# Stores on POOL's queue, gate weights a chunk ahead, four gate buffers in the merge: a one-core transformer block

## The chip, the core and the metric

The kernel runs on one core of one Trainium2 chip. A core has a matrix engine (TensorE, here PE, with its weight loads shown as PEld), three elementwise engines (VectorE = DVE, ScalarE = ACT, GpSimd = POOL) and a fifth that issues transfers only (SyncE = SP). Each engine takes its own instructions strictly in order; engines wait for each other on semaphores. Transfers (DMAs) are issued by an engine, in its order, and then run beside it. The metric is device time in microseconds for one execution, lower is better.

## The reference, cut to what matters

One block on x of 512 positions by 1024 channels, all in float32:

```python
h = rmsnorm(x, norm_mix_g)
z = h @ w_in                                   # 1024 x 7184
uv = gelu(z[:, :2048]); z_u, z_v = uv[:, :1024], uv[:, 1024:]
q, k, v, f_logit = ...                         # 3 x 1024 columns, then 16
gates = sigmoid(z[:, 5136:])                   # gate_a, gate_b: 1024 columns each
a = z_u * (W_s @ layernorm(z_v) + b_s)         # W_s: 8 groups, 128 x 128, inside blocks of 128 positions
b = forgetting_attention(q, k, v, f_logit)     # 16 heads; cum = cumsum(log_sigmoid(f_logit + b_f))
x = x + (gate_a * (a @ w_branch_a) + gate_b * (b @ w_branch_b)) @ w_out
x = x + (gelu(conv(h2 @ w_up)[:, :2816]) * conv(h2 @ w_up)[:, 2816:]) @ w_down   # h2 = rmsnorm(x)
x = x + (p @ w_ple) * sigmoid(rmsnorm(x) @ w_ple_gate)
return rmsnorm(x)
```

## The kernel before, in words

**Products.** Every float32 product is made of three products of rounded parts. `load_w` loads a weight tile of 128 x 1024 floats into a raw buffer (L141, a DMA issued by SP), ACT casts it to its high part `whi` (L144), and DVE, or POOL where `sub=G`, subtracts that to get the low part `wlo` (L145). `split_out` does the same to a result (L366 on ACT, L367 on DVE). A product then runs three matmuls per 128 rows: `wlo` with the high part of the activation (L167, L153, L227, L299 are the first of three in their product functions), and two more.

**Buffers.** Raw weights go in turn through a ring of three buffers `raw` and, until the attention, five more called `more`. The high and low parts have rings of their own. A load is issued when its buffer is free.

**Stages.** (1) Norm of x; V, first half; the forget gate's logits (L568, 16 matmuls) from a weight that is cast by DVE (L561) and whose low part DVE makes (L562); V, second half. The cumulated log of the forget gate goes to DRAM (`cum_d`, L591), and comes back in the attention, spread over partitions. DVE and ACT also form four sums of quarters of h (L607 and splits into S1 to S4), for the next stage. (2) A chunk of gates (`gate_steps(0)`: 24 matmuls, then ACT copies the result and a store puts it into `gate_d`, L642), then z_v and z_u by two Winograd-Strassen products of seven quarter products each (P1, P7, P6, P2, P5, P4, P3; L299 to L306), whose weight quarters are loaded by L267 and combined on DVE (L272). (3) The mix: one gate chunk as cover, and then eight groups `mix(g)`: split of the normalised z_v, three matmuls, product with z_u (L724), four transposes (L729), split into the halves of S4h or S4l in turn, and two stores to `aT_d` (L733); between them, as fill, the matmuls of three more gate chunks. (4) The attention over eight pairs of heads, with the q and k of later pairs and nine more gate chunks as fill. POOL clears two K tiles (kz, L772 and L773) and adds the mask to `cum` (md, L804). (5) The merge: for each chunk of the b branch, load gate (L967), sigmoid (L968), product, multiply (L980), store to `gyb_d` (L981); then the a branch likewise (multiply L991), with the stored b part loaded (L993), added on POOL (L994) and split into mT. Gate tiles have two buffers `sg`. (6) w_out, the feed-forward part, the end.

**What sets the order.** On PE it is the order of the code in these stages (`manual_schedule`), with `weave` putting fill between items. On the other engines a list scheduler with its own estimate of times orders the instructions, so that a change in one place may move instructions elsewhere.

Of the kernel before, what the change touches and what calls it, by code (L numbers as in the profile page):

```python
# [9 lines left out]
F32 = mybir.dt.float32  # L10
F32R = mybir.dt.float32r
AF = mybir.ActivationFunctionType
# [3 lines left out]
P = 128  # L16
S = 512
# [26 lines left out]
def hybrid_block(  # L44
# [27 lines left out]
    def uid(s):  # L72
        state["n"] += 1
        return f"{s}_{state['n']}"
# [55 lines left out]
    def more_tile():  # L130
        return state["more"].tile([P, D], F32, tag="more", name=uid("more"), bufs=X_BUFS)
# [104 lines left out]
    def steps(g, n):  # L236
        for _ in range(n):
            next(g)
# [349 lines left out]
    V.tensor_tensor(fbb[:, 1:, :], fbb[:, 1:, :], tot[0:16, 0:15, None].broadcast_to([16, 15, 32]),  # L588
                    ALU.add)
    cum_d = tc.dram_tile([16, S], F32, name="cum_d")  # L590
    nc.sync.dma_start(cum_d, fb)  # L591


    maskb = consts.tile([P, P], F32, tag="maskb", name="maskb")
# [37 lines left out]
    def gate_weights(n):  # L632
        return load_w(w_in_v[:, :, gate_col(n):gate_col(n) + P], 8, P)

    def gate_steps(n, tag, place, w=None):

        w = w or gate_weights(n)
        bk = bank(tag)
        yield from proj_T_steps([(*w, 0, 8, 0)], hT, bk)
        t = place()  # L640
        A.copy(t, bk)
        nc.sync.dma_start(gate_d[n * P:n * P + P, :], t)  # L642
# [19 lines left out]
    def chain(*gs):  # L662
        for g in gs:
            yield from g
# [1 line left out]
    bsT = ph.tile([P, NK], F32, tag="bsT", name="bsT")  # L666
    aT_d = [tc.dram_tile([D, S], F32, name=f"aT_d{t}") for t in range(2)]
    with tc.manual_schedule(engines={ET.PE}):
        run(gate_steps(0, "mm", lambda: more_tile()[:, 0:512]))
        units = wino_steps(wino_jobs(w_in_v, 1024, hT, sums, wino_rows(zv, gelu_zv))  # L670
                           + wino_jobs(w_in_v, 0, hT, sums, wino_rows(zu, gelu_zu)))
        steps(units, 168)
        gb = [more_tile(), more_tile()]
        nc.sync.dma_start(gb[0], rows_bc(ln_g[0], D))
        nc.sync.dma_start(gb[1], rows_bc(ln_b[0], D))

        wst = more_tile().rearrange("p (g s) -> p g s", g=8)
        nc.sync.dma_start(wst, w_s[0].rearrange("g t s -> t g s"))
        G.memset(wst[0:64, :, 64:128], 0.0)
        bsr = ph.tile([P, P], F32, tag="bsr", name="bsr")  # L680
        G.memset(bsr, 0.0)
        nc.sync.dma_start(bsr[0:8, :], b_s[0])
        steps(units, 24)

        nm, va = tiny("nm", NB), tiny("va", NB)
        V.tensor_tensor(nm, zs[:, 0:NB], zs[:, NB:], ALU.add)
        V.tensor_scalar(nm, nm, -1.0 / D, None, ALU.mult)
        sq = tiny("sq", 2 * NB, 1)
        for rb in range(NB):
            A.activation(zv[:, rb, :], zv[:, rb, :], AF.Identity, bias=nm[:, rb:rb + 1])  # L690
            for h in range(2):
                A.activation(bank("mm"), zv[:, rb, 512 * h:512 * h + 512], AF.Square,
                             accum_out=sq[:, NB * h + rb:NB * h + rb + 1])
        V.tensor_tensor(va, sq[:, 0:NB], sq[:, NB:], ALU.add)
        V.tensor_scalar(va, va, 1.0 / D, EPS, ALU.mult, ALU.add)
        y = rsqrt_of(va, NB)
        for rb in range(NB):
            V.scalar_tensor_tensor(zv[:, rb, :], zv[:, rb, :], y[:, rb:rb + 1], gb[0],
                                   ALU.mult, ALU.mult)
            V.tensor_tensor(zv[:, rb, :], zv[:, rb, :], gb[1], ALU.add)  # L700
        steps(units, 120)

        wsT = [quarter(f"S1{t}").rearrange("p (g t) -> p g t", g=8) for t in "hl"]
        bk = bank("mm")
        T.transpose(bk[:, 0:P], bsr, ident)
        V.tensor_copy(bsT, bk[:, 0:NK])
        steps(units, 12)
        for g0 in (0, 4):
            bk = bank("mm")
            for g in range(4):  # L710
                T.transpose(bk[:, g * P:(g + 1) * P], wst[:, g0 + g, :], ident)
            split_out(wsT, bk.rearrange("p (g t) -> p g t", g=4),
                      (slice(None), slice(g0, g0 + 4), slice(None)))
            steps(units, 6)

        def mix(g):
            c = slice(g * P, g * P + P)
            vp = quarter(f"S2{'hl'[g % 2]}").rearrange("p (t b c) -> p t b c", t=2, b=NB)
            vh, vl = vp[:, 0], vp[:, 1]
            split_out((vh, vl), zv[:, :, c], (slice(None),) * 3)  # L720
            bk = bank("sc")
            mm3(bk, wsT[0][:, g, :], wsT[1][:, g, :], vh, vl, True, True)
            an = quarter(f"S3{'hl'[g % 2]}", F32)[:, 0:512].rearrange("p (b c) -> p b c", b=NB)
            V.scalar_tensor_tensor(an, bk.rearrange("p (b c) -> p b c", b=NB), bsT[:, g:g + 1],  # L724
                                   zu[:, :, c], ALU.add, ALU.mult)
            yield
            bk = bank("pt")
            for n in range(NB):
                T.transpose(bk[:, n * P:(n + 1) * P], an[:, n, :], ident)  # L729
            ap = quarter(f"S4{'hl'[g % 2]}").rearrange("p (t r) -> p t r", t=2)  # L730
            split_out((ap[:, 0], ap[:, 1]), bk, (slice(None),) * 2)
            for t in range(2):
                nc.sync.dma_start(aT_d[t][g * P:g * P + P, :], ap[:, t].bitcast(F32))  # L733
            yield

        run(units)
        for n in range(N_FIRST, N_FIRST + N_COVER):
            run(gate_steps(n, "mm", lambda: more_tile()[:, 0:512]))
        ms = [mix(g) for g in range(NK)]
        items = [ms[0], ms[1]]  # L740
        for g in range(2, NK):
            items += [ms[g - 2], ms[g]]
        items += [ms[NK - 2], ms[NK - 1]]
        w_qk = []

        def preload(g):

            next(g)
            yield
            w_qk.extend(qk_weights(pr) for pr in range(2))  # L750
            yield from g

        fill = [gate_steps(n, "mm", lambda: more_tile()[:, 0:512]) for n in range(GATES[0] - 1 - N_MIX, GATES[0] - 1)]
        fill = chain(*fill[:-1], preload(fill[-1]))
        weave(items, fill, 24 * N_MIX)
        run(fill)

# [175 lines left out]
    state["bank"] = 0  # L933
    with tc.manual_schedule(engines={ET.PE}):
        run(gate_steps(N_GATES - 1, None,
                       lambda: scr.tile([P, S], F32, tag="gy", name=uid("gt"), bufs=2), w_merge[0]))
    for k0 in (0, 4):
        for t in range(2):
            nc.sync.dma_start(aT[t][:, k0:k0 + 4, :].bitcast(F32),
# [18 lines left out]
        return cvT[:, P + 44 + c:P + 45 + c]  # L958


    def gated(wv, act, n0, py=None):

        c0 = P * (n0 % NK)
        sgs = []
        for i in range(2):
            sg = scr.tile([P, S], F32, tag="sg", name=uid("sg"), bufs=2)
            nc.sync.dma_start(sg, gate_d[(n0 + i) * P:(n0 + i + 1) * P, :])  # L967
            A.activation(sg, sg, AF.Sigmoid)  # L968
# [9 lines left out]
    for c0 in range(0, D, 256):  # L978
        for by, sg, c in gated(w_b_v, oT, c0 // P, None if c0 else w_merge[1]):
            V.tensor_tensor(sg, by, sg, ALU.mult)  # L980
            nc.sync.dma_start(gyb_d[c * P:c * P + P, :], sg)  # L981

    bk = bank()
    for i in range(2):
# [4 lines left out]

    def store_a(by, sg, c):  # L990
        V.tensor_tensor(sg, by, sg, ALU.mult)  # L991
        gy = scr.tile([P, S], F32, tag="gy", name=uid("gy"), bufs=2)
# [4 lines left out]
    for c0 in range(0, D, 256):  # L997
        for y in gated(w_a_v, aT, NK + c0 // P):
            store_a(*y)

    scr_es.close()

# [232 lines left out]
```

## Time and profile before

| | |
|---|---|
| runs | 992.82, 993.49 and 996.77 us, median 993.49 |
| the profiled execution | 993.0 us, of which the span of its instructions is 991.2 us |
| granted TensorE clock, mean over the span | 0.985 |
| busy: PE, DVE, ACT, POOL | 945.1, 597.6, 465.5, 113.7 us |
| longest wait of PE in all | 17.2 us on L145, in 3 waits |
| DMA | 121.21 MB, nearly all issued by SP; none by POOL |

A row of the timeline gives start and duration in us, engine, line, operation, output <- inputs, shape, and in brackets how long the engine idled before it and what ended that. "x2" groups neighbours. Rows marked SPq are instructions of SP's queue, which only issue. A row of waits gives the sum, how often, and the longest. A row of windows gives the stretch, the busy time of each engine, the granted clock (1.00 is full speed), the DMA engines' mean share and GB/s.

### The profile page before, as it was taken

The numbers are of one execution on the slowest core, as the hardware profiler recorded it, in microseconds if no ns is written. First come the engines' busy times: TensorE is split into PE (matmuls) and PEld (weight loads), VectorE is DVE, ScalarE is ACT, GpSimd is POOL, SyncE is SP. The second block draws the span as 40 slices with busy tenths as digits, with TensorE's granted clock in tenths as the row PEclk, the third lists the DMA queues.
The fourth block names the chain that finished last, engine by engine and source line by source line (L and its number), as shares of the span: only waits on it lengthen the run. The fifth ranks groups of instructions, "written<-read, shape, count | busy, mean of one in ns | idle before, by whom it ended". The sixth has DMA issues, their size and how long they took to land.

```text
span 991.2 us, 11717 instructions
## 1 busy us (share of the span) xinstructions
PE 945.1 (95%) x4375; PEld 779.5 (79%) x4375; DVE 597.6 (60%) x1017; ACT 465.5 (47%) x779; POOL 113.7 (11%) x94
## 2 busy tenths in 40 slices
PE   8998998679999999999998999999999999999996
PEld 6776886568888887788886788888888888888885
DVE  6838887446777788543346656655346663355664
ACT  7634673337666666443234454443224442144443
POOL 3000000005322201000022300000000000000225
PEclk9999999889999999999999999999999999999998
DMA  9222451365333332259855233333323333223212
GB/s 343 77 80 91 154 149 32 128 204 178 87 106 98 105 106 75 65 169 332 284 173 191 63 126 106 109 106 95 97 64 106 95 117 107 85 86 106 71 36 85
DMA packets 102148, 121.21 MB, mean 122 GB/s; under 512 B 5252, under 2 KB 70972, under 8 KB 102092
## 3 DMA queue, kind: packets, MB, share of 16 engines
q1 hardware_dynamic: 101948, 120.21, 38.0%
q8 instruction: 34, 0.56, 0.2%
q10 hardware_dynamic: 144, 0.26, 0.1%
q14 instruction: 22, 0.18, 0.1%
HBM read 106.79 MB, written 13.66 MB: 122 GB/s over the span
## 4 chain that ended last, share of the span: by engine, by line
PE 75%; DMA 10%; DVE 8%; ACT 3%; issue 2%; POOL 1%; SPq 0%; POOLq 0%; ACTq 0%; DVEq 0%
PE bank L167 14%; PE bank L169 13%; PE bank L171 13%; PE bank L153 5%; PE bank L154 5%; PE bank L155 5%; DMA sg<-gate_d 4%; PE bank L227 3%; PE bank L231 3%; PE bank L229 3%; DMA gyb_d<-sg 2%; PE bank L303 2%; PE bank L306 2%; PE bank L299 2%; PE bank L856 2%
## 5 line engine op out<-in xcount | busy, mean ns | idle before, releaser
L167 PE MATMUL bank<-slot,wlo 128*128 128x512 f32 (+1 forms) x744 | 296.8, 400 | 18.1 <-DVE wlo L145 17.2
L169 PE MATMUL bank<-slot,whi 128*128 128x512 f32 (+1 forms) x744 | 290.1, 390 | 0.0
L171 PE MATMUL bank<-slot,whi 128*128 128x512 f32 (+1 forms) x744 | 289.9, 390 | 0.0
L144 ACT CAST whi<-raw 128x1024 fp32r<-128x1024 f32 x130 | 135.5, 1046 | 112.7 <-PE bank L155 67.9
L145 DVE TENSOR_TENSOR wlo<-raw,whi 128x1024 fp32r<-128x1024 f32 x108 | 136.3, 1266 | 85.0 <-ACT whi L144 84.7
L167 PEld LDWEIGHTS bank<-slot,wlo 128*128 128x128 f32 x744 | 140.8, 189 | 44.0 <-DVE wlo L145 15.0
L171 PEld LDWEIGHTS bank<-slot,whi 128*128 128x128 f32 x744 | 140.4, 189 | 29.2
L169 PEld LDWEIGHTS bank<-slot,whi 128*128 128x128 f32 x744 | 140.9, 189 | 22.4
L145 POOL TENSOR_TENSOR wlo<-raw,whi 128x1024 fp32r<-128x1024 f32 x22 | 53.9, 2453 | 543.5 <-ACT whi L144 543.5
L153 PE MATMUL bank<-whi,slot 128*128 128x512 f32 (+1 forms) x232 | 89.4, 386 | 3.5 <-DVE slot L367 3.5
L154 PE MATMUL bank<-wlo,slot 128*128 128x512 f32 (+1 forms) x232 | 89.2, 384 | 0.0
L155 PE MATMUL bank<-whi,slot 128*128 128x512 f32 (+1 forms) x232 | 89.0, 384 | 0.0
L227 PE MATMUL bank<-whi,slot 128*128 128x512 f32 x152 | 59.9, 395 | 2.6 <-DVE slot L367 2.6
L231 PE MATMUL bank<-whi,slot 128*128 128x512 f32 x152 | 59.6, 392 | 0.0
L229 PE MATMUL bank<-wlo,slot 128*128 128x512 f32 x152 | 59.2, 390 | 0.0
L153 PEld LDWEIGHTS bank<-whi,slot 128*128 128x128 f32 x232 | 44.0, 190 | 12.5 <-DVE slot L367 3.9
L155 PEld LDWEIGHTS bank<-whi,slot 128*128 128x128 f32 x232 | 44.0, 190 | 8.7
L154 PEld LDWEIGHTS bank<-wlo,slot 128*128 128x128 f32 x232 | 44.0, 190 | 8.5
L1075 DVE SCALAR_TENSOR_TENSOR ul<-bank,cvT,ul 128x511 f32<-128x511 f32 x22 | 16.5, 750 | 51.3 <-ACT ul L1074 51.3
L829 ACT ACTIVATE t<-t,mn 128x512 f32<-128x512 f32 (+1 forms) x64 | 35.9, 561 | 10.9 <-DVE mn L826 8.1
L366 ACT CAST pth<-bank 128x512 fp32r<-128x512 f32 (+1 forms) x64 | 26.3, 428 | 24.9 <-PE bank L847 24.7
L1012 DVE TENSOR_TENSOR slot<-bank,slot 128x512 f32<-128x512 f32 x32 | 21.7, 687 | 23.3 <-PE bank L155 13.8
(274 smaller groups left out, 1359.8 us busy)
## 6 DMA issues: line engine op xcount, KB each, us to landing
raw<-in_w_up_dram SPq DMA_DIRECT2D x44, 512.0 KB, 3.6
raw<-in_w_in_dram SPq DMA_DIRECT2D x36, 512.0 KB, 5.2
raw<-in_w_down_dram SPq DMA_DIRECT2D x22, 512.0 KB, 3.3
more<-in_w_in_dram SPq DMA_DIRECT2D x20, 512.0 KB, 4.7
cum<-cum_d SPq DMA_DIRECT2D x8, 512.0 KB, 4.4
raw<-in_w_branch_b_dram SPq DMA_DIRECT2D x8, 512.0 KB, 3.7
slot<-aT_d SPq DMA_DIRECT2D x4, 1024.0 KB, 12.3
sg<-gate_d SPq DMA_DIRECT2D x16, 256.0 KB, 4.3
```

Of the source, the lines that this page charges most:

```text
L144: A.copy(hi, raw)
L145: (sub or V).tensor_tensor(lo, raw, hi.bitcast(F32), ALU.subtract)
L153: T.matmul(out_ap, alo, bhi, start=start, stop=False)
L154: T.matmul(out_ap, ahi, blo, start=False, stop=False)
L155: T.matmul(out_ap, ahi, bhi, start=False, stop=stop)
L167: T.matmul(out_ap, wl, ah, start=(n == 0 and k == 0), stop=False)
L169: T.matmul(out_ap, wh, al, start=False, stop=False)
L171: T.matmul(out_ap, wh, ah, start=False, stop=end)
L227: T.matmul(bk, alo[:, k, r], wh, start=(k == 0), stop=False)
L229: T.matmul(bk, ahi[:, k, r], wl, start=False, stop=False)
L231: T.matmul(bk, ahi[:, k, r], wh, start=False, stop=(k == nk - 1))
L829: A.activation(t, t, AF.Exp, scale=-1.0, bias=m, accum_out=rs[:, i:i + 1])
```

## The change

It has five parts.

1. The stores to `cum_d`, of gate chunks 0 to 4, to `aT_d` and to `gyb_d` are issued by POOL in place of SP. The gate stores of the attention stay on SP.
2. The output of gate chunks 0 to 4 gets two buffers of its own (`gt`), where it took one of the five `more` buffers.
3. The weights of gate chunk n + 1 are loaded at the start of chunk n, and those of the first two pairs of heads at the start of chunk 4.
4. In the merge, gate tiles have four buffers (`sg`) and the `gy` tiles three; the gates of a pair of chunks are loaded a pair ahead, and the sigmoid stands just before each product.
5. The sum of the two branches is made by DVE in place of POOL.

```diff
     cum_d = tc.dram_tile([16, S], F32, name="cum_d")
-    nc.sync.dma_start(cum_d, fb)
+    G.dma_start(cum_d, fb)
...
+    def gate_tile():
+        return ph.tile([P, S], F32, tag="gt", name=uid("gt"), bufs=2)
+
-    def gate_steps(n, tag, place, w=None):
+    def gate_steps(n, tag, place, w=None, queue=nc.sync):
...
-        nc.sync.dma_start(gate_d[n * P:n * P + P, :], t)
+        queue.dma_start(gate_d[n * P:n * P + P, :], t)
...
-        run(gate_steps(0, "mm", lambda: more_tile()[:, 0:512]))
+        run(gate_steps(0, "mm", gate_tile, None, G))
...
-                nc.sync.dma_start(aT_d[t][g * P:g * P + P, :], ap[:, t].bitcast(F32))
+                G.dma_start(aT_d[t][g * P:g * P + P, :], ap[:, t].bitcast(F32))
...
+        first, ahead, w_qk = N_FIRST, [gate_weights(N_FIRST)], []
+
+        def mix_gates():
+            for n in range(first, GATES[0] - 1):
+                w = ahead.pop()
+                if n + 1 < GATES[0] - 1:
+                    ahead.append(gate_weights(n + 1))
+                else:
+                    w_qk.extend(qk_weights(pr) for pr in range(2))
+                yield from gate_steps(n, "mm", gate_tile, w, G)
+
         run(units)
-        for n in range(N_FIRST, N_FIRST + N_COVER):
-            run(gate_steps(n, "mm", lambda: more_tile()[:, 0:512]))
+        fill = mix_gates()
+        steps(fill, 24 * N_COVER)
...
-        fill = [gate_steps(n, "mm", lambda: more_tile()[:, 0:512]) for n in range(GATES[0] - 1 - N_MIX, GATES[0] - 1)]
-        fill = chain(*fill[:-1], preload(fill[-1]))
         weave(items, fill, 24 * N_MIX)
...
-    def gated(wv, act, n0, py=None):
-        c0 = P * (n0 % NK)
+    def gates_of(n):
         sgs = []
         for i in range(2):
-            sg = scr.tile([P, S], F32, tag="sg", name=uid("sg"), bufs=2)
-            nc.sync.dma_start(sg, gate_d[(n0 + i) * P:(n0 + i + 1) * P, :])
-            A.activation(sg, sg, AF.Sigmoid)
+            sg = scr.tile([P, S], F32, tag="sg", name=uid("sg"), bufs=4)
+            nc.sync.dma_start(sg, gate_d[(n + i) * P:(n + i + 1) * P, :])
             sgs.append(sg)
-        py = py or pieces_T(wv, c0)
-        for i in range(2):
-            by = bank()
-            proj_T(py[i], act, by)
-            yield by, sgs[i], c0 // P + i
+        return sgs
+
+    def branch(wv, act, n0, use, sgs, py=None):
+        for n in range(0, NK, 2):
+            nxt = gates_of(n0 + n + 2) if n0 + n + 2 < N_GATES else None
+            py = py or pieces_T(wv, P * n)
+            for i in range(2):
+                A.activation(sgs[i], sgs[i], AF.Sigmoid)
+                by = bank()
+                proj_T(py[i], act, by)
+                use(by, sgs[i], n + i)
+            sgs, py = nxt, None
+        return sgs
...
+    def store_b(by, sg, c):
+        V.tensor_tensor(sg, by, sg, ALU.mult)
+        G.dma_start(gyb_d[c * P:c * P + P, :], sg)
...
-        G.tensor_tensor(sg, sg, gy, ALU.add)
+        V.tensor_tensor(sg, sg, gy, ALU.add)
```

In the changed kernel the lines behind these shift: the gate store is L645, the aT_d stores L736, kz L777 and L778, md L809, the gate loads of the merge L971, its multiplies L991 (b) and L1004 (a), its sum L1007.

Three places in the order of the instructions. The first is DVE in stage (1), round the forget gate's weight (S4l is its raw tile, S2l its parts; zv holds the transposed h there). Before:

```order
L607 TENSOR_TENSOR zv_96<-zv_96 128x4x256
L562 TENSOR_TENSOR S2l_445<-S4l_444,S2l_445 128x8x16
L367 TENSOR_TENSOR slot_35_137<-bank_370,slot_35_137 128x8x64
L607 TENSOR_TENSOR zv_96<-zv_96 128x4x256
L367 TENSOR_TENSOR S1l_494<-zv_96,S1h_493 128x1024
L145 TENSOR_TENSOR wlo_523<-more_521,whi_522 128x1024
L607 TENSOR_TENSOR zv_96<-zv_96 128x4x256
L367 TENSOR_TENSOR S3l_498<-zv_96,S3h_497 128x1024
L145 TENSOR_TENSOR wlo_529<-raw_527,whi_528 128x1024
L145 TENSOR_TENSOR wlo_535<-raw_533,whi_534 128x1024
```

and now:

```order
L367 TENSOR_TENSOR S1l_494<-zv_96,S1h_493 128x1024
L561 CAST S2l_445<-S4l_444 128x512
L145 TENSOR_TENSOR wlo_523<-more_521,whi_522 128x1024
L607 TENSOR_TENSOR zv_96<-zv_96 128x4x256
L367 TENSOR_TENSOR S3l_498<-zv_96,S3h_497 128x1024
L145 TENSOR_TENSOR wlo_529<-raw_527,whi_528 128x1024
L562 TENSOR_TENSOR S2l_445<-S4l_444,S2l_445 128x8x16
L145 TENSOR_TENSOR wlo_535<-raw_533,whi_534 128x1024
```

The cast L561, which stood ahead of the second L607, and the low part L562 have moved behind the V split, the splits of S1l and S3l, and two weight splits.

The second is SP in the mix. Before (L141 are weight loads, all else stores):

```order
L642 DMA gate_d<-more_1349 128x512
L733 DMA aT_d_653<-S4h_1391 128x512
L733 DMA aT_d_654<-S4h_1391 128x512
L733 DMA aT_d_653<-S4l_1419 128x512
L733 DMA aT_d_654<-S4l_1419 128x512
L141 DMA more_1442<-in_w_in_dram 128x8x128
L642 DMA gate_d<-more_1439 128x512
L733 DMA aT_d_653<-S4h_1457 128x512
```

and now:

```order
L141 DMA more_1318<-in_w_in_dram 128x8x128
L141 DMA more_1324<-in_w_in_dram 128x8x128
L141 DMA more_1367<-in_w_in_dram 128x8x128
L141 DMA more_1448<-in_w_in_dram 128x8x128
L141 DMA more_1530<-in_w_in_dram 128x8x128
L141 DMA raw_1821<-in_w_in_dram 128x8x128
L141 DMA raw_1884<-in_w_in_dram 128x8x128
```

The loads of the mix's gate weights and of the first pair's now follow each other, with no store between them.

The third is POOL where the attention begins; before, its queue had nothing between a memset in stage (2) and the split `wlo_1886`. Now:

```order
L736 DMA aT_d_653<-S4l_1617 128x512
L736 DMA aT_d_654<-S4l_1617 128x512
L645 DMA gate_d<-gt_1627 128x512
L145 TENSOR_TENSOR wlo_1886<-raw_1884,whi_1885 128x1024
L777 MEMSET kz_1638 64x512
L778 MEMSET kz_1638 64x512
```

The last of the 20 stores of the mix stand right ahead of the split and the memsets that the attention's beginning needs.

More of the change, by code (lines that the diff above doesn't have):

```diff
@@ L743, in hybrid_block @@
         items += [ms[NK - 2], ms[NK - 1]]
[L744 to L751, printed above, removed]
-        fill = [gate_steps(n, "mm", lambda: more_tile()[:, 0:512]) for n in range(GATES[0] - 1 - N_MIX, GATES[0] - 1)]
-        fill = chain(*fill[:-1], preload(fill[-1]))
         weave(items, fill, 24 * N_MIX)
@@ L935, in hybrid_block @@
         run(gate_steps(N_GATES - 1, None,
-                       lambda: scr.tile([P, S], F32, tag="gy", name=uid("gt"), bufs=2), w_merge[0]))
+                       lambda: scr.tile([P, S], F32, tag="gy", name=uid("gt"), bufs=3), w_merge[0]))
     for k0 in (0, 4):
@@ L958, in cb @@
         return cvT[:, P + 44 + c:P + 45 + c]
-    def gated(wv, act, n0, py=None):
-        c0 = P * (n0 % NK)
+    def gates_of(n):
         sgs = []
         for i in range(2):
-            sg = scr.tile([P, S], F32, tag="sg", name=uid("sg"), bufs=2)
-            nc.sync.dma_start(sg, gate_d[(n0 + i) * P:(n0 + i + 1) * P, :])
-            A.activation(sg, sg, AF.Sigmoid)
+            sg = scr.tile([P, S], F32, tag="sg", name=uid("sg"), bufs=4)
+            nc.sync.dma_start(sg, gate_d[(n + i) * P:(n + i + 1) * P, :])
             sgs.append(sg)
-        py = py or pieces_T(wv, c0)
-        for i in range(2):
-            by = bank()
-            proj_T(py[i], act, by)
-            yield by, sgs[i], c0 // P + i
+        return sgs
[10 more added lines that the diff above has]
+        return sgs
     gyb_d = tc.dram_tile([D, S], F32, name="gyb_d")
[L978 to L981, printed above, removed]
+    def store_b(by, sg, c):
+        V.tensor_tensor(sg, by, sg, ALU.mult)
+        G.dma_start(gyb_d[c * P:c * P + P, :], sg)
+    sgs = branch(w_b_v, oT, 0, store_b, gates_of(0), w_merge[1])
     bk = bank()
@@ L991, in store_a @@
         V.tensor_tensor(sg, by, sg, ALU.mult)
-        gy = scr.tile([P, S], F32, tag="gy", name=uid("gy"), bufs=2)
+        gy = scr.tile([P, S], F32, tag="gy", name=uid("gy"), bufs=3)
         nc.sync.dma_start(gy, gyb_d[c * P:c * P + P, :])
-        G.tensor_tensor(sg, sg, gy, ALU.add)
+        V.tensor_tensor(sg, sg, gy, ALU.add)
         split_out(mT, sg, (slice(None), c, slice(None)))
-    for c0 in range(0, D, 256):
-        for y in gated(w_a_v, aT, NK + c0 // P):
-            store_a(*y)
+    branch(w_a_v, aT, NK, store_a, sgs)
     scr_es.close()
```

## The prediction

> **What bounds the kernel now.** I read, in this order, the busy times, what PE waited for, stretches of the span, and then the rows of each engine's timeline round each wait.
>
> ```profile
> PE 945.1 (95%) x4375; PEld 779.5 (79%) x4375; DVE 597.6 (60%) x1017; ACT 465.5 (47%) x779; POOL 113.7 (11%) x94
> ```
>
> PE is busy for 945.1 of the 991.2 us. The change touches no product, so what it can win is PE's idle time, about 46 us, and the time that PE runs slowly after idling. Who it waited for (sum, times, longest):
>
> ```profile
> PE bank L167 <- DVE wlo L145: 17.2, 3, 7.4
> PE bank L153 <- DVE slot L367: 3.5, 1, 3.5
> PE bank L299 <- ACT whi L250: 2.9, 2, 1.6
> PE bank L303 <- DVE wlo L251: 1.6, 2, 0.8
> ```
>
> The first line is three gate chunks of the mix that wait for a split weight; the second the product of w_out waiting for the last split of the merge; the last two the first Winograd products. In the stretches, PE's busy time and granted clock (PEclk) show the same places:
>
> ```profile
> 74.00:86.00 12.00, 8.12 (x25) 5.75 (x25) 8.28 (x8) 4.32 (x6) 0.00 (x0) 0.86 0.45 154
> 167.00:187.00 20.00, 10.87 (x42) 8.53 (x43) 8.62 (x12) 5.52 (x9) 0.00 (x0) 0.82 0.33 106
> 187.00:205.00 18.00, 10.61 (x44) 8.40 (x43) 6.00 (x8) 5.00 (x8) 0.00 (x0) 0.78 0.51 160
> 520.00:540.00 20.00, 16.53 (x67) 13.23 (x66) 14.53 (x14) 10.10 (x15) 4.22 (x3) 0.91 0.60 198
> ```
>
> A wait costs more than itself. Behind the 3.01 us wait of the mix, PE's rows read:
>
> ```profile
> 169.36 0.52 PE L167 MATMUL bank<-slot,wlo 128*128 128x512 f32 x1 [3.01 <-DVE wlo L145]
> 169.68 0.63 PE L169 MATMUL bank<-slot,whi 128*128 128x512 f32 x1
> ...
> 173.07 0.40 PE L167 MATMUL bank<-slot,wlo 128*128 128x512 f32 x1
> 173.31 0.39 PE L169 MATMUL bank<-slot,whi 128*128 128x512 f32 x1
> 173.54 0.39 PE L171 MATMUL bank<-slot,whi 128*128 128x512 f32 x1
> ```
>
> From 169.68 to 173.07 eight matmuls start, 0.424 us apart; from 173.31 on they start 0.23 us apart (0.227 over longer undisturbed runs). A wait of this length thus costs eight times 0.20, 1.6 us, on top.
>
> **The mix: stores leave SP, weights come a chunk ahead.** SP's rows show the cause of the second wait, and ACT's row what came of it:
>
> ```profile
> 175.02 1.61 SPq L733 DMA_DIRECT2D aT_d<-S4h  x2
> 178.22 1.04 SPq L733 DMA_DIRECT2D aT_d<-S4l  x2
> 179.37 0.39 SPq L141 DMA_DIRECT2D more<-in_w_in_dram  x1
> 184.06 1.04 ACT L144 CAST whi<-more 128x1024 fp32r<-128x1024 f32 x1 [3.73 <-DMA more<-in_w_in_dram]
> ```
>
> SP takes its queue in order. The load of the next gate weight stands behind four stores that wait for ACT and DVE; it goes out at 179.37, its cast starts at 184.06, the low part follows, and PE gets it after 6.77 us of waiting. In the changed order no store is left on SP there, and the weights of chunks 2 to 4 and of the first pair of heads are loaded, and four of them split, before or at the start of the mix. I take all three waits away: −17.2, and three slow stretches at 1.6: −4.8. Next late is what the order puts ahead of the first chunk on DVE, one more split of a weight at the pitch of these rows:
>
> ```profile
> 152.25 1.22 DVE L145 TENSOR_TENSOR wlo<-more,whi 128x1024 fp32r<-128x1024 f32 x1
> 153.38 1.22 DVE L700 TENSOR_TENSOR zv<-zv,more 128x1024 f32<-128x1024 f32 x1
> ```
>
> DVE runs without a gap from there to the split for which PE waits at 159.93, so PE's start moves by 1.13: +1.1. Two more splits behind it delay the first item of the mix by 3.4 altogether, still inside the 5.5 us (24 matmuls at 0.227) that chunk 1 covers.
>
> The cost is POOL's: 16 aT_d and 4 gate stores in the shortened mix, some 33 us (127 matmuls at 0.227 and eight groups of transposes at 0.35 make 31.6, and the last group's evacuation follows). No DMA issued by POOL is in this trace. Its price per store is bounded below by SP's (1.04 us for two, above: 0.52) and above by POOL's own dearest work:
>
> ```profile
> 221.05 2.49 POOL L145 TENSOR_TENSOR wlo<-raw,whi 128x1024 fp32r<-128x1024 f32 x1 [80.29 <-ACT whi L144]
> 223.61 0.52 POOL L772 MEMSET kz<- 64x512 f32 x1
> ```
>
> 20 × 0.52 is 10 us and hides; 20 × 2.49 is 50 us and costs 17. POOL limits the mix from 33/20 = 1.65 us per store. I take 1.0, nearer to SP's row since it is an issue and not elementwise work: hidden. The landing counts too, because ACT writes S4h and S4l again two groups later (2 × 3.1 us) and then waits for the store:
>
> ```profile
> ACT S4l L366 <- DMA aT_d<-S4l: 5.7, 1, 5.7
> ...
> aT_d<-S4h SPq DMA_DIRECT2D x8, 256.0 KB, 3.7
> aT_d<-S4l SPq DMA_DIRECT2D x8, 256.0 KB, 2.3
> ```
>
> Cast 0.6, split 0.7, issue 1.0 and landing 3.7 give 6.0 of 6.2 us. It is nearly tight, so I add +1.0 (0 if it lands like S4l; 3 × 2 = +6 at two us more, three reuses of each buffer).
>
> The Trainium skill ("SBUF — State Buffer", § Who interferes with whom) speaks against these stores: descriptors of a DMA issued by GpSimd are written by GpSimd itself, which a VectorE operation in a two-port mode locks out. By it each store could wait for DVE's operation in progress. In rows, that is up to the 1.22 us of a split: 20 × (0.52 + 1.22) = 35 us, about +2 here. The trace cannot show it. The page "DMA: Bandwidth & Descriptors" (§ Issuing engines are not separate DMA queues) says that a second issuing engine only saves the sequencer's issue time; by that the mix would win 20 × 0.52 of SP's time and hardly any of PE's. The rows of 175.02 to 184.06 disagree: what the load lost was SP's waiting behind stores, and the DMA share of those stretches was 0.33 and 0.51. I follow the rows.
>
> **The beginning: gate 0 and the first Winograd products.**
>
> ```profile
> 58.48 0.93 SPq L267 DMA_DIRECT2D more<-in_w_in_dram  x2
> 74.12 0.34 SPq L642 DMA_DIRECT2D gate_d<-more  x1
> 74.51 2.26 SPq L267 DMA_DIRECT2D more<-in_w_in_dram  x3
> ...
> 67.87 0.39 PE L167 MATMUL bank<-slot,wlo 128*128 128x512 f32 x1
> ...
> 91.42 0.39 PE L299 MATMUL bank<-whi,S2l 128*128 128x512 f32 x1
> ```
>
> SP stands from 59.4 to 74.12 behind the store of gate 0, with three loads behind that. From gate 0's first matmul to that of the third product (91.42) there are 72 matmuls: 16.4 us at 0.227, and it took 23.55. With the store gone, and gate 0's output no longer in a buffer that these loads need, all these loads stand ahead: −7.1.
>
> But the order shows a new thing. The cast and the low part of the forget gate's weights (L561, L562) stand far later on DVE: between the first addition L607 and the low part now stand three more L607, a split of V, those of S1l and S3l and two of weights.
>
> ```profile
> 36.77 0.42 DVE L561 CAST S2l<-S4l 128x512 fp32r<-128x512 f32 x1
> 37.10 1.22 DVE L607 TENSOR_TENSOR zv<-zv 128x1024 f32<-128x1024 f32 x1
> 38.24 0.28 DVE L562 TENSOR_TENSOR S2l<-S4l,S2l 128x128 fp32r<-128x128 f32 x1
> ...
> 42.41 3.84 PE L568 MATMUL bank<-slot,S2l 128*64 128x512 f32 x16
> ...
> 44.72 2.35 DVE L145 TENSOR_TENSOR wlo<-raw,whi 128x1024 fp32r<-128x1024 f32 x2
> ```
>
> Before, L562 was done at 38.5 and PE came to L568 at 42.41 without a wait. Now DVE goes from 36.77, where L561 stood, through seven operations of 1024 columns at the pitch of 1.14 (37.10 to 38.24), V's split at 0.6 and L561 itself at 0.33: 8.9 us. L562 begins at 45.7 and ends at 45.9 (the two weight splits, now at 41 and 44.5, stood at 41 and 44.72 before, so their casts are there). PE stands 3.5 us, a wait of the length that brought the slow eight, so +1.6: with that +5.1. Nothing fills in: PE's order is written by hand. All that follows starts later, the Winograd products too, with their loads long landed, so the two add up: −2.0 for this part. The cum_d store on POOL holds DVE's split behind it (S4l, 1.7 us waited before); PE is then in 22 us of V products, which hides several us more.
>
> **The attention's start.** On POOL the stores stand ahead of a split (2.49), four memsets at 0.58 pitch and the first mask sum, and ACT's first scores now stand behind a memset. Those memsets came 7.4 us after the mix's last transposes (216.2); PE first asks for a result of theirs near 10. I put +0.6 (0 to 3).
>
> **The merge.** The chain waits here for gate loads, and ACT most of all:
>
> ```profile
> ACT sg L968 <- DMA sg<-gate_d: 44.7, 15, 7.0
> ...
> 514.25 0.39 PE L153 MATMUL bank<-whi,slot 128*128 128x512 f32 x1
> ...
> 531.11 0.69 DVE L991 TENSOR_TENSOR sg<-bank,sg 128x512 f32<-128x512 f32 x1 [2.19 <-ACT sg L968]
> ```
>
> PE finishes the a branch at 514.25 and has three quarters of the first half of w_out (72 matmuls, 16.4 us) before it needs the last split; but the last gate product runs at 531.11, since two gate buffers are reloaded in turn. With four, loaded a pair (10.9 us of PE) ahead, product, sum (0.69 on DVE), cast and split follow the branch in about 3.2 us, far inside 16.4. That takes the 3.5 and its eight slow matmuls: −5.1. The eight sums on DVE are 5.5 us, hidden by a DVE that has 14.5 us of work in the 20 of 520 to 540; with POOL's sums goes the slowing of splits beside them:
>
> ```profile
> 522.04 2.06 DVE L145 TENSOR_TENSOR wlo<-raw,whi 128x1024 fp32r<-128x1024 f32 x1 [0.17 <-ACT whi L144]
> ```
>
> (1.22 elsewhere). The gyb_d stores, two per 10.9 us, are free on POOL at any price above. The feed-forward part and the end keep their order: 0.
>
> **Sum.** +5.1 − 7.1 − 17.2 − 4.8 + 1.1 + 1.0 + 0.6 − 5.1 = −26.4. Against the profiled execution, 993.0 us (span 991.2 and 1.8 around it), that is 966.6. The median shown is 993.49, 0.5 above it; I predict 967.
>
> **The rivals.**
> - POOL's stores hold the mix. For it: no price in the trace, and the turn of S4h and S4l with 0.2 us to spare. Against it: POOL has nothing else there. At 2.0 us a store, 40 − 33 = +7: 974; at 2.49, +17: 983.
> - The forget gate does not wait: L561 and L562 come early enough. For it: DVE's place is an order, and its waits could be shorter; against it: every operation ahead has a row with its duration. Without the 5.1: 961.5.
> - The change does not do what it says in one place: loads and stores share the DMA engines, and a weight (or the last gates of the merge) still lands late. Against it: DMA shares of 0.33 to 0.60. One wait of 6.8 with its 1.6, or the merge's 5.1, stays: 972 to 975.
> - It does not do so in the whole mix, because transfers and not SP's order make the weights late: the 22.0 of the mix stay, 989. Against it stand the four stores between SP's two loads, each behind an evacuation. The rule on issuing engines would have it so.
> - Slower: POOL's stores cost so much that the mix takes longer than now. From (33 + 26.4)/20 = 3.0 us each the whole gain is gone; at 3.5 the mix takes 70 us, 37 more than its 33: 967 + 37 = 1004. Only the missing price speaks for it; against it, it lies above the dearest POOL row here.
>
> **How the numbers follow.** My forecast (963 to 971) has 0.56, the held mix 0.21, the forget gate hidden 0.11, a load still late 0.05, all of the mix's late 0.02, slower 0.05. The likeliest gives 967; the range reaches down to the hidden forget gate with a little more (960) and up to stores at 2.49 us (983). About 0.5%, 5 us, is what a measurement can tell from no change. The whole mix late falls within it, and a price close to 3 us: same 0.03; slower 0.05; faster 0.92.
>
> **What would show it.** In the changed profile: a wait of PE L568 on DVE L562 of about 3.5 us near 42 and slow matmuls behind it; no wait on L145 in the mix, and a clock near 1.00 from 160 to 195; none on L251 and whi near 75 to 90; no wait of the w_out product on L367; POOL's issues in the mix with their length, which is the price I lack. The prediction fails if ACT waits for S4h and S4l in every group, or if DVE, with four splits more before the mix, brings the V normalisation late by more than 1.1 us.

## The result, and the profile after

The changed kernel takes 964.66 us (963.84 to 965.79), the kernel before 994.06 in the same comparison: a ratio of 0.9701, 95% interval 0.9678 to 0.9725. The profiled execution takes 964.26 us, its span is 962.5. The prediction was 967 (960 to 983).

The busy times on the page, and what PE waited for longest (sum, times, longest):

```profile
PE 936.6 (97%) x4375; PEld 774.9 (81%) x4375; DVE 596.9 (62%) x1025; ACT 465.6 (48%) x779; POOL 118.4 (12%) x116
```

```profile
PE bank L568 <- DVE S2l L562: 3.5, 1, 3.5
PE bank L852 <- DVE ptl L367: 3.2, 3, 1.7
PE bank L227 <- DVE slot L367: 2.6, 2, 1.4
PE bank L714 <- DVE bsT L709: 2.0, 1, 2.0
```

The span is 28.7 us shorter. PE's idle time fell from 46.1 to 25.9 (20.2), its busy time from 945.1 to 936.6 (8.5): the same 4375 matmuls, fewer of them at the slow clock. Gone from the list are the waits on L145, on L251 and whi, and on the last split of the merge; L568 on L562 is new, and the wait for bsT has grown from 0.9.

The same stretches of the changed kernel (PE's busy time first, the granted clock behind the POOL column); the mix is now in 160 to 191:

```profile
42.00:60.00 18.00, 14.46 (x57) 10.23 (x56) 12.31 (x15) 8.39 (x11) 0.00 (x0) 0.91 0.38 118
74.00:86.00 12.00, 12.00 (x55) 9.94 (x54) 5.69 (x6) 5.69 (x8) 0.58 (x1) 1.00 0.07 23
160.00:191.00 31.00, 31.00 (x151) 25.57 (x150) 23.22 (x31) 13.88 (x22) 9.16 (x17) 1.00 0.55 184
500.00:520.00 20.00, 20.00 (x90) 16.55 (x89) 6.04 (x9) 7.38 (x14) 2.39 (x1) 1.00 0.29 98
```

From the starts of matching matmuls in the two timelines, each stage's length in us:

| from, to | before | after | difference | predicted |
|---|---|---|---|---|
| L568's first matmul comes at | 42.41 | 46.16 | +3.75 | +3.5 |
| L568, to V's second half | 3.68 | 5.31 | +1.63 | +1.6 |
| gate 0, to the third Winograd product | 23.55 | 16.33 | −7.2 | −7.1 |
| transposed bias, to gate chunk 1 | 8.66 | 9.79 | +1.1 | +1.1 |
| gate chunk 1, to the mix's last transposes | 55.92 | 31.89 | −24.0 | −21.0 |
| there, to the first scores | 11.92 | 12.93 | +1.0 | +0.6 |
| these two rows together | 67.84 | 44.82 | −23.0 | −20.4 |
| w_out's first matmul, to its second half | 27.09 | 21.76 | −5.3 | −5.1 |

The mix's last transposes do not stand at the same place in both kernels: from gate chunk 1 on, 159 matmuls come ahead of them before and 153 now, so six fill matmuls (1.4 us at 0.227) have moved from the one row to the next; PE's order is not fixed by the code alone there. The two rows together hold the same 212 matmuls in both, and in the changed kernel PE does not idle in them.

The price that the trace of before could not show is in POOL's timeline of the changed kernel (four of the mix's stores), and in its table of issues (count, KB each, us to landing):

```profile
169.75 0.54 POOL L736 DMA_DIRECT2D aT_d<-S4h  x1 [3.30 <-ACT S4h L366]
170.57 0.54 POOL L736 DMA_DIRECT2D aT_d<-S4h  x1 [0.28 <-DVE S4h L367]
172.96 0.54 POOL L736 DMA_DIRECT2D aT_d<-S4l  x1 [1.85 <-ACT S4l L366]
173.68 0.54 POOL L736 DMA_DIRECT2D aT_d<-S4l  x1 [0.18 <-issue]
```

```profile
aT_d<-S4h POOLq DMA_DIRECT2D x8, 256.0 KB, 2.8
aT_d<-S4l POOLq DMA_DIRECT2D x8, 256.0 KB, 3.0
```

Each holds POOL 0.54 us and lands in about 3. Twenty are 10.8 us of the 31.9.

### The profile page after: what moved, and what is told of

Same layout as the page of the kernel before. It is cut to its first block, busy times and chain, and to the rows that moved or that the text cites. A ratio compares the mean times of both kernels' runs of the same rounds, so it can differ in the third digit from the quotient of the medians.

```text
span 962.5 us, 11722 instructions
## 1 busy us (share of the span) xinstructions
PE 936.6 (97%) x4375; PEld 774.9 (81%) x4375; DVE 596.9 (62%) x1025; ACT 465.6 (48%) x779; POOL 118.4 (12%) x116
## 4 chain that ended last, share of the span: by engine, by line
PE 88%; DVE 6%; ACT 2%; issue 1%; DMA 1%; POOL 1%; SPq 0%; POOLq 0%; DVEq 0%
PE bank L167 17%; PE bank L169 17%; PE bank L171 17%; PE bank L153 5%; PE bank L155 5%; PE bank L154 5%; PE bank L227 3%; PE bank L229 3%; PE bank L231 3%; PE bank L306 2%; PE bank L303 2%; PE bank L299 2%; PE bank L861 2%; PE bank L852 1%; PE bank L403 1%
## 5 line engine op out<-in xcount | busy, mean ns | idle before, releaser
L145 DVE TENSOR_TENSOR wlo<-raw,whi 128x1024 fp32r<-128x1024 f32 x108 | 132.6, 1229 | 109.2 <-ACT whi L144 108.8
L145 POOL TENSOR_TENSOR wlo<-raw,whi 128x1024 fp32r<-128x1024 f32 x22 | 53.8, 2449 | 518.7 <-ACT whi L144 511.1
L155 PEld LDWEIGHTS bank<-whi,slot 128*128 128x128 f32 x232 | 43.6, 188 | 8.5
L153 PEld LDWEIGHTS bank<-whi,slot 128*128 128x128 f32 x232 | 43.6, 188 | 8.5
L227 PEld LDWEIGHTS bank<-whi,slot 128*128 128x128 f32 x152 | 28.6, 188 | 8.9 <-DVE slot L367 3.4
```

The source lines that it names most:

```text
L145: (sub or V).tensor_tensor(lo, raw, hi.bitcast(F32), ALU.subtract)
L153: T.matmul(out_ap, alo, bhi, start=start, stop=False)
L155: T.matmul(out_ap, ahi, bhi, start=False, stop=stop)
L227: T.matmul(bk, alo[:, k, r], wh, start=(k == 0), stop=False)
```

## The experiments

The first four runs ask which of the parts carries the mix and the beginning. Three take one part each and put it alone into the kernel before; the fourth takes away the new wait.

### Own gate tiles alone

```diff
# before
-        run(gate_steps(0, "mm", lambda: more_tile()[:, 0:512]))
+        run(gate_steps(0, "mm", gate_tile))       # and likewise chunks 1 to 4
```

> The kernel before with one edit: the output of gate chunks 0 to 4 gets two buffers of its own, all stores stay on SP, no load a chunk ahead, the merge as before. In its order the mix's weight loads stand ahead of all aT_d stores on SP, and the forget gate's low part has moved back on DVE as in the changed kernel. Theory A (what matters is that the loads stand ahead of the stores in SP's order, by whatever means): the mix's three waits go (-23 with their slow stretches), the beginning gives -1.8 (+5.4 for the wait of L568, -7.2 for the Winograd start), the merge keeps its 5.3: 994 - 25 = 969. Rival B (the stores have to leave SP): only the beginning changes, 992. Rival C (the DMA engines' load makes weights late): 985 to 994.

968.62 us against 993.64 (ratio 0.975, 0.9721 to 0.9779). The stage from gate chunk 1 to the first scores, 67.84 before and 44.82 in the changed kernel, takes 44.78. SP's rows in the mix (loads L141, stores L736):

```profile
151.35 3.77 SPq L141 DMA_DIRECT2D more<-in_w_in_dram  x3
...
170.79 1.16 SPq L736 DMA_DIRECT2D aT_d<-S4h  x2
173.96 1.05 SPq L736 DMA_DIRECT2D aT_d<-S4l  x2
```

The last of the mix's gate weights goes out at about 155, ahead of all aT_d stores, which stay on SP. Theory A holds and rivals B and C fall: the stores need not leave SP. This one edit also brings the whole of the beginning (16.32 from gate 0 to the third product) and the new wait of 3.5 on L562: the Winograd loads come early because gate 0 no longer takes one of their buffers, and the scheduler then puts L561 and L562 late.

That the sum came to 969 is partly luck. The beginning won 1.0 us and not 1.8. The merge, which was to keep its 5.3, gave 4.2 of them: PE's wait for its last split is 0.8 here, although the merge and the order of its instructions are those of before. The attention took 2.7 us more.

### Stores on POOL alone

```diff
# before: queue=G for gate chunks 0 to 4, and
-    nc.sync.dma_start(cum_d, fb)
+    G.dma_start(cum_d, fb)
-                nc.sync.dma_start(aT_d[t][g * P:g * P + P, :], ap[:, t].bitcast(F32))
+                G.dma_start(aT_d[t][g * P:g * P + P, :], ap[:, t].bitcast(F32))
```

> The kernel before with the stores of cum_d, of gate chunks 0 to 4 and of aT_d on POOL, nothing else: gate outputs stay in the weights' buffers, no load a chunk ahead, the merge as before. In its order the mix's loads stand together on SP, and the forget gate's cast keeps its early place. Theory A: the mix's waits go, -23; no wait of L568; the third Winograd load of the first product still needs the buffer of gate chunk 0, so P7's wait (about 2 us of 7.2) stays, -4: 967. Rival D (a buffer is what the loads lacked): the weights of chunks 3 and 4 land late, one or two waits of 5 to 9 us stay: 976 to 985.

984.09 us against 993.64 (0.9901, 0.9873 to 0.9929). The same stage takes 61.87, 6 less than before, not 23. Theory A missed by 17 us, and the trace says why; three waits of one kind remain, each of 3.0 us or a little less. The rows of PE, ACT and DVE round the first:

```profile
167.73 0.47 PE L167 MATMUL bank<-slot,wlo 128*128 128x512 f32 x1 [3.00 <-DVE wlo L145]
...
164.13 0.59 ACT L641 COPY more<-bank 128x512 f32<-128x512 f32 x1 [3.43 <-PE bank L171]
165.28 1.04 ACT L144 CAST whi<-more 128x1024 fp32r<-128x1024 f32 x1
...
166.36 1.22 DVE L145 TENSOR_TENSOR wlo<-more,whi 128x1024 fp32r<-128x1024 f32 x1 [0.24 <-ACT whi L144]
```

The weight is there: no cast of the mix waits for a DMA any more. But ACT has the cast of the next chunk's weight behind the copy of this chunk's output, and only then come cast (1.04) and split (1.22), with PE idle. That is an order on ACT, not on SP, and neither theory A nor rival D had it, though the time lies in D's range. The trace of before shows the same for its first wait (ACT's rows):

```profile
165.76 0.59 ACT L641 COPY more<-bank 128x512 f32<-128x512 f32 x1 [3.43 <-PE bank L171]
166.39 0.62 ACT L366 CAST S2h<-zv 128x512 fp32r<-128x512 f32 x1
166.91 1.04 ACT L144 CAST whi<-more 128x1024 fp32r<-128x1024 f32 x1
```

No DMA is named there. The wait of 3.01 was this order from the beginning, and the waits of 6.77 and 7.39 were the same turn of 3 us with a late load in it, for which ACT waited 3.73 and 4.41.

Part of what the mix won is lost behind it, to something new. ACT's first operation of the attention starts when the store of the last gate chunk, out of a `more` buffer, has landed, and PE waits behind it:

```profile
ACT st L787 <- DMA gate_d<-more: 4.0, 1, 4.0
```

```profile
PE bank L167 <- DVE st L788: 2.5, 1, 2.5
```

PE's waits in the stage thus fall from 17.2 to 11.3, which is the 6. Of the Winograd start 3.2 us of waits on whi and L251 stay as well (21.89 from gate 0 to the third product).

### Loads a chunk ahead alone

```diff
# before: mix_gates() as in the change, outputs still in more_tile(), stores on SP
-        for n in range(N_FIRST, N_FIRST + N_COVER):
-            run(gate_steps(n, "mm", lambda: more_tile()[:, 0:512]))
+        fill = mix_gates()
+        steps(fill, 24 * N_COVER)
```

> The kernel before with the gate weights beside the mix loaded one chunk ahead, nothing else: stores on SP, gate outputs in the weights' buffers. In its order the loads of chunks 2 and of one more stand ahead of the stores, those of chunk 4 and of the first pair of heads behind four and nine stores. Theory A: the first wait (3.0 and 1.6) goes, of the two others one goes or both get shorter since the load that stands behind stores is now asked for a chunk earlier: 975 to 985. Rival E (loading a chunk ahead is the whole effect): 971. Rival (it has no effect): 994.

974.45 us against 993.64 (0.9806, 0.9774 to 0.9839), just below the range of theory A and above the 971 of rival E. The stage takes 45.69. Here loads do stand behind stores on SP; the cast of the last gate weight waits for its load:

```profile
188.85 1.05 ACT L144 CAST whi<-more 128x1024 fp32r<-128x1024 f32 x1 [1.66 <-DMA more<-in_w_in_dram]
```

Yet PE waits on no L145: a weight asked for a chunk early is split before PE needs it, late load or not. For the mix that is rival E, and more than theory A allowed. The profiled executions of this run and of own tiles alone lie 3.4 us apart. The stage makes 0.9 of that and all ahead of it 0.5; the merge makes 4.2 (w_out's stretch is 27.19 here and 22.94 there), though neither edit touches it, and the attention gives 2.3 back.

### The forget gate's weight in a buffer of its own

```diff
# after
-    wf_raw = fm[1][:, 512:].rearrange("p (k c) -> p k c", k=8)
+    wf_raw = ph.tile([P, S], F32, tag="gt", name=uid("gt"), bufs=2).rearrange("p (k c) -> p k c", k=8)
```

> The changed kernel with one edit: the raw weight of the forget gate goes into a buffer of its own (one of the two gate output tiles, free at that time) and so is loaded, cast and split at the beginning. Theory: L568's wait of 3.5 us and its slow matmuls (together 5.4 from before's place of the V products) go and nothing takes their place: 964.7 - 5.4 = 959.3. Rival: the wait moves to the next thing, the weight splits of V's second half or the first Winograd products: 961 to 965.

959.43 us (958.41 to 960.05) against 993.64, ratio 0.966 (0.9637 to 0.9683). DVE's rows of that kernel:

```profile
21.99 1.09 DVE L561 CAST S2l<-gt 128x512 fp32r<-128x512 f32 x1
23.78 0.28 DVE L562 TENSOR_TENSOR S2l<-gt,S2l 128x128 fp32r<-128x128 f32 x1
```

The buffer is one of the two `gt` buffers, which no gate chunk uses yet. PE comes to L568 at 42.00 without a wait, and everything behind is 5.6 to 5.8 us earlier than in the changed kernel. The wait moves nowhere. The changed kernel had paid these 5 us for its early loads without need; of all versions that were run, none is faster than this by more than the runs can tell.

### The rest of that kernel with every store back on SP

```diff
# the run before, and
-    G.dma_start(cum_d, fb)
+    nc.sync.dma_start(cum_d, fb)             # gate chunks 0 to 4, aT_d and gyb_d likewise
```

> The kernel of the run before (forget gate's weight in its own buffer: 959.4 us) with the stores to cum_d, to gate_d of chunks 0 to 4, to aT_d and to gyb_d back on SP; own gate tiles, load a chunk ahead, four gate buffers and DVE's sum stay. Theory now (buffers and early loads carry the gain, POOL's queue nothing): 959.4, within 1.5. Rival (POOL's queue still matters once the rest is there, in the mix or the merge): 962 to 970.

960.01 us against 995.19, ratio 0.9659 (0.9634 to 0.9683), as against 0.966 with POOL. Once weights come early, POOL's queue is worth nothing that these runs can tell (each interval reaches 2.4 us to either side). This is also what the Trainium skill says ("DMA: Bandwidth & Descriptors", § Issuing engines are not separate DMA queues): a second issuing engine saves issue time only. The kernel before is another case: there loads stood behind stores in SP's order, and POOL's stores alone won 1.7 us at the Winograd start and 6.0 from gate chunk 1 to the first scores.

### The merge with two gate buffers, and with POOL's sum

```diff
# after, first run
-            sg = scr.tile([P, S], F32, tag="sg", name=uid("sg"), bufs=4)
+            sg = scr.tile([P, S], F32, tag="sg", name=uid("sg"), bufs=2)
# after, second run
-        V.tensor_tensor(sg, sg, gy, ALU.add)
+        G.tensor_tensor(sg, sg, gy, ALU.add)
```

> The changed kernel with two buffers for the gates of the merge in place of four; loads are still asked for a pair ahead, but can only start when a buffer is free. Theory of the prediction: PE's wait before the last quarter of w_out (3.5, and 1.6 of slow matmuls) is back: 969.8. Rival (the wait came from a chance of timing, as the run with own tiles alone hints, where the old merge waited 0.8): 964.7 to 967.

> The changed kernel with the sum of the branches on POOL again (1.3 us each, up to 2.3 beside DVE). Theory: with four gate buffers the last split follows the a branch by about 4.5 us in place of 3.2, far inside the 16.4 that w_out's first three quarters cover: 964.7, within 1. Rival (POOL's sum was what held the chain): a wait of 2 to 5 us in the w_out product, 967 to 970.

966.45 us (0.9719, 0.9687 to 0.9751) and 963.84 (0.9695, 0.9667 to 0.9723), both against 995.19. Neither has a wait of w_out on the last split; the stretch of w_out is 22.19 and 21.76, where the changed kernel has 21.76. The theory of the prediction, that four buffers are needed, falls with the first run, though there the last split comes only just in time. The next three runs go the other way and add one part each to the kernel before.

### Four gate buffers alone, DVE's sum alone, a pair ahead alone

```diff
# before, three runs
+            sg = scr.tile([P, S], F32, tag="sg", name=uid("sg"), bufs=4)
# or
+        V.tensor_tensor(sg, sg, gy, ALU.add)
# or gates_of() and branch() of the change, with two buffers, POOL's sum and SP's stores
```

> The kernel before with four buffers for the gates of the merge, nothing else. Theory (the two buffers, reloaded in turn, set the pace of the a branch's gate products): the wait of 3.5 and its slow matmuls go: 994 - 5 = 989. Rival (the loads still stand too late in SP's order, behind the gyb_d stores): a wait of 2 to 3.5 stays, 992 to 994.

> The kernel before with the sum of the branches on DVE, nothing else. Theory: POOL's sum (1.3 to 2.3 us) is one link of the chain load, sigmoid, product, sum, split that frees a gate buffer; with DVE's 0.7 each of the last four turns gets about 1 us shorter: the wait falls from 3.5 to under 1: 990. Rival (the loads, not the sum, hold the chain): unchanged, 994.

> The kernel before with the gates of the merge asked for a pair ahead in the code and the sigmoid just before each product, with two gate and two gy buffers, POOL's sum and SP's stores as before. Theory (a load can only start when a buffer is free, so asking earlier changes nothing): the wait stays, 993 to 995. Rival (the order of the loads on SP and of the sigmoids on ACT is what counts, as the changed kernel with two buffers hints, where no wait was left): 989.

Against 995.5: 990.18 (0.9957, 0.9939 to 0.9976), 990.77 (0.996, 0.9938 to 0.9982), 996.05 (1.0008, 0.9985 to 1.003). The first two have no wait there (w_out's stretch 21.76 in both, 27.09 before); the third has

```profile
PE bank L153 <- DVE slot L367: 4.3, 1, 4.3
```

and a stretch of 29.13. So the wait hung on one chain, load, sigmoid, product, sum, split, turning on two buffers. Its last gate product starts 16.9 us behind w_out's first matmul in the kernel before and 17.7 with the pair ahead alone. DVE's sum, shorter by 0.6 to 1.6 us in each turn, brings that to 11.5, and to 14.1 in the changed kernel with two buffers. Four buffers bring it to 1.0, and to 0.2 in the changed kernel, where the product waits for PE and no longer for a sigmoid:

```profile
490.27 0.39 PE L153 MATMUL bank<-whi,slot 128*128 128x512 f32 x1
...
490.47 0.69 DVE L1004 TENSOR_TENSOR sg<-bank,sg 128x512 f32<-128x512 f32 x1 [0.41 <-PE bank L171]
```

Asking earlier, with no buffer free, does nothing by itself. The 5.3 of the merge were to be had from either of two lines. How long the wait is does not hang on the merge's code alone: with that code unchanged it is 3.5 before and with the loads ahead, 0.8 with own tiles and 1.7 with POOL's stores, where the last gate product comes 14.2 and 15.1 behind. Why the chain runs up to 2.7 us earlier there, no run shows.

### Four times the stores on POOL

```diff
# after
             for t in range(2):
-                G.dma_start(aT_d[t][g * P:g * P + P, :], ap[:, t].bitcast(F32))
+                for r in range(0, S, P):
+                    G.dma_start(aT_d[t][g * P:g * P + P, r:r + P], ap[:, t, r:r + P].bitcast(F32))
```

> The changed kernel with each store to aT_d cut into four by columns (64 in place of 16). If each keeps POOL 0.54 us (as the 20 stores of the changed kernel do), a former store costs 2.16, above the 1.65 from which POOL should bound the mix: 68 x 0.54 = 36.7 against 31.9, so +5 in the mix, and more where POOL's split and memsets for the attention stand behind: 970 to 974. Rival (the issue costs POOL by the amount of data, 0.14 each): no change, 964.7.

984.83 us against 995.19 (0.991, 0.988 to 0.9939). POOL's rows (x8 is 8 issues), and two of PE's waits in that stretch:

```profile
171.23 4.26 POOL L737 DMA_DIRECT2D aT_d<-S4h  x8 [3.30 <-ACT S4h L366]
175.48 4.26 POOL L737 DMA_DIRECT2D aT_d<-S4l  x8
...
203.52 4.27 POOL L737 DMA_DIRECT2D aT_d<-S4l  x8
```

```profile
PE bank L167 <- DVE st L794: 7.2, 1, 7.2
PE bank L825 <- POOL kz L778: 3.8, 1, 3.8
```

Each issue of 64 KB holds POOL 0.53, as those of 256 KB held it 0.54: the price goes by issues. To its last transposes the mix takes 36.90, 5.0 more, the number worked out. That is partly chance: 167 matmuls come ahead of these transposes and not 153, which is 3.2 us, and PE waits only 1.7 in that stretch. The forecast missed by 11 us because of what follows: POOL is then still more than 20 us behind (its last store of the mix goes out near 222, the last transposes start at 197.6), and its split and its memsets for the attention come that much later: from there to the first scores 20.69 instead of 12.93, and 5.8 more in the attention.

### The bias copy on ACT

```diff
# the kernel of 959.43, and
-        V.tensor_copy(bsT, bk[:, 0:NK])
+        A.copy(bsT, bk[:, 0:NK])
```

> The kernel with the forget gate's weight in its own buffer (959.4 us) and one edit more: the copy of the transposed bias b_s (bsT), for which PE waits 2.0 us right before the mix, is made by ACT, which is idle there, in place of DVE. Theory: the wait of 2.0 goes, and PE's next wait (on the split of S1l, 0.8, which is DVE's) grows by half of it: 958.4. Rival (DVE is the bound there, all of it is given back at the split): 959.4.

960.33 us against 995.5 (0.9651, 0.9625 to 0.9676), as against 0.966 without the edit: no gain that can be told, which is what the rival said. PE's rows without and with the edit:

```profile
150.73 0.66 PE L714 MATMUL bank<-ident,more 128*128 128x128 f32 x4 [2.05 <-DVE bsT L709]
153.60 0.50 PE L167 MATMUL bank<-slot,wlo 128*128 128x512 f32 x1 [0.82 <-DVE S1l L367]
```

```profile
153.97 0.51 PE L167 MATMUL bank<-slot,wlo 128*128 128x512 f32 x1 [3.01 <-DVE S1l L367]
```

DVE, which has no gap there, sets the start of the mix. Two short waits became one of 3.0, and the one long wait was followed by a slow stretch (33.42 in place of 31.82 to the mix's last transposes) that the two short ones did not bring.

## Why the prediction was right, and where it was wrong

- **The beginning: right in its terms, and half right on their cause.** L562 began at 45.82 (45.7 worked out), PE waited 3.54 (3.5), the V products started 5.4 late (5.1). The Winograd start gave back 7.2 (7.1). DVE's row, counted through nine operations with their durations in the trace of before:

```profile
45.82 0.28 DVE L562 TENSOR_TENSOR S2l<-S4l,S2l 128x128 fp32r<-128x128 f32 x1
```

For the Winograd start it named two reasons together, the store gone from SP and the buffer that gate 0 no longer takes. The second does it: own tiles alone, with the store on SP, bring all of it (16.32), POOL's stores alone little (21.89, where kernels that leave this stage alone took 23.55 to 26.2).
- **The mix: right in size, wrong in its cause.** The waits went, as forecast, with their slow stretches; the size was met because the change also has the two parts that cure the other cause. The step that failed is the reading of SP's queue as the one cause. Two things had to be in time, the load, and the cast on ACT behind the gate's copy. The store's queue cures the first alone and leaves three waits of 3; own tiles or a load a chunk ahead cure both. The row of ACT that shows it was in the trace of before, and the prediction quoted only a cast that did wait for a DMA.
- **+1.1 ahead of the mix: right** (9.79 − 8.66).
- **The landing, +1.0, and the attention's start, +0.6: nothing came of either.** ACT did wait once for a store, 1.5 us, and PE did not see it:

```profile
ACT S4h L366 <- DMA aT_d<-S4h: 1.5, 1, 1.5
```

The +1.0 that the table shows for the attention's start is six matmuls that moved there. From the first gate chunk to the first scores the change gives 23.0, where the terms −22.0, +1.0 and +0.6 make −20.4. Of the 2.6 between them 1.6 are these two terms, and the rest is in the slow stretches, which the prediction put at 4.8. The stage before, less its 17.2 of waits and the 44.8 of the changed kernel, leaves 5.8. Their size isn't fixed: the same sum gives 4.3, 5.9 and 4.1 in the three other kernels that left the mix alone, with waits of 17.0 to 17.4.
- **POOL's price: 1.0 taken, 0.54 measured**, at the lower of the two bounds given (0.52, SP's row). The choice by likeness, issue work and not elementwise work, was right. Its threshold of 1.65 a former store was tried at one point only: at 2.13 the kernel lost 20 us, more behind the mix than in it. Nothing of a locked-out descriptor writer shows: the issues are 0.54 each beside a DVE that is busy for 23 of 31 us. The prediction priced that rule with a split of 1.22 us, and a split is a TENSOR_TENSOR. The section that it cites (the Trainium skill, "SBUF — State Buffer", § Who interferes with whom) says that `tensor_tensor` has no two-port mode, so neither that price nor these stores beside DVE's splits test the rule.
- **The merge: right in size, and right that its chain turns on the gate buffers**; that four are needed was not: two do, if the sum is DVE's (the run with two gate buffers, and DVE's sum alone).

## What to carry to other kernels

When a load looks late, read also where its consumer stands in its own engine's order: the cast behind the copy was half of these waits (9 us of 17.2), and moving stores to another queue did not touch it. Give the output that shares a ring with weights a buffer of its own before looking for another queue; here that alone did in the mix what three parts were there for. And read the order of every engine after a change, not only at the edit: here early loads came with two small operations pushed behind four and seven others, which cost 5 us and took one line to win back. A stage cut at an instruction that moves does not compare equal work; cut it where both kernels have done the same.

## What the runs showed of the hardware that was not expected

What a wait costs in clock is not fixed. PE's rows at L568 behind practically the same wait in three kernels, the changed one, the one with POOL's sum, and own tiles alone (16 matmuls each):

```profile
46.16 5.47 PE L568 MATMUL bank<-slot,S2l 128*64 128x512 f32 x16 [3.54 <-DVE S2l L562]
```

```profile
46.10 3.89 PE L568 MATMUL bank<-slot,S2l 128*64 128x512 f32 x16 [3.55 <-DVE S2l L562]
```

```profile
46.03 6.44 PE L568 MATMUL bank<-slot,S2l 128*64 128x512 f32 x16 [3.55 <-DVE S2l L562]
```

Without a wait they take 3.84. So, in the order of the rows, 3.55 us of idling cost 1.6, 0 and 2.6 us more; the granted clock from 42 to 54 was 0.86, 1.00 and 0.72. The runs with two gate buffers and with four times the stores paid 2.6 as well. The Trainium skill ("TensorE: Matmul & The Clock Gate", § What's actually happening) describes activity that is watched in free-running windows of about 3.4 us; a wait that falls differently across two windows would do this. The runs show the spread, not the windows. The prediction's 1.6 a wait is the middle of what there is.
